# Trace of a batched matrix product: the last batch's twelve rows of A in two loads, and more of the last B on TensorE

## The chip, the core and the metric

The kernel runs on one core of a Trainium2 chip. The metric is the device time in microseconds, the median over several executions. TensorE is called PE here, VectorE DVE, ScalarE ACT, GpSimd POOL and SyncE SP, as the profile calls them.

## The reference

```python
B, N = 8, 2176
a, b: (B, N, N) float32, standard normal

prod = np.matmul(a, b)
traces = np.diagonal(prod, axis1=1, axis2=2).sum(axis=-1)     # (8,) float32
```

The trace of a product is the sum over i and j of a[i, j] * b[j, i]. So no product of matrices has to be made: A is transposed and multiplied element by element with B, and everything is summed. Both inputs must be read whole, 303 MB.

## The kernel before

**Tiles.** N = 2176 is 17 times 128. A "row" below is one of 17 blocks of 128 rows of a matrix. In SBUF a matrix lies as 128 partitions by 17 rows by 2176 columns in bf16; the loads cast from float32. The rows come in three groups: two of six (`SIX`) and one of five (`FIVE`). The tile `five` holds the five rows 12 to 16, first of A and then of B; `a_six` and `b_six` hold the twelve rows 0 to 11 of A and of B; `at` holds A transposed. Within a group of m rows, partition p holds m successive rows of the matrix, so that a load reads one long stretch of memory for each partition and group.

**Loads.** POOL issues nearly all of them, in this order for each batch: A's five rows (`d_a5`), A's twelve (`d_a6`, both groups of six in one DMA), B's five (`d_b5`) and B's twelve (`d_b6`). It waits before each for its buffer to be free: `product` counts DVE's multiplications, `made` counts the tiles that PE has transposed. The last batch's B comes in nine pieces instead (`pieces`), so that the work on it can follow the loads closely: piece 0 is the five rows 12 to 16, piece 1 the rows 0 to 5, piece 2 the rows 6 and 7, pieces 3 to 5 the rows 8, 9 and 10, and pieces 6 to 8 parts of row 11. Each has a semaphore of its own (`d_late`).

**Transposing A.** `tiles` lists the steps: eight for the five rows (`HEAD` is 8), nine for each group of six. A step is up to 16 transposes on PE into one of three slots of PSUM, which ACT (three steps of four) or DVE (each fourth) then copies into `at`. PE runs the steps of all batches in one hardware loop (L217). It waits on the semaphore `moved` ahead of the five rows' first step and ahead of the twelve rows' first. SP posts to `moved`: it waits for the loads `d_a5` and `d_a6` of each batch in turn and adds one for each. So PE's loop needs no waits on counts that change from batch to batch.

**Multiplying.** In batches 0 to 6 DVE multiplies `at` with B and sums, in one instruction for the five rows and one for the twelve (L285, `multiply_reduce`). In the last batch the work is divided between DVE and PE by the list `shares`, with one entry (lo, hi, more) for each piece: DVE multiplies the elements lo to hi, PE takes the rest in steps of 128 columns, as matmuls that add up in `trace_ps` (L254) and whose diagonal is wanted. `more` is a number of extra matmuls of 128x512 into a PSUM slot whose results are not used (L256). PE goes through the pieces in order and waits for each piece's load; it begins once all of A is evacuated. DVE does its parts in order (from L318), each into a column of `late`, then waits for PE's last matmul (`added`), reduces the diagonal of `trace_ps` into a further column (the instruction that writes `diagonal`), PE adds the columns (L334), DVE copies the result (L339) and SP stores it.

Of the kernel before, what the change touches and what calls it, by code (L numbers as in the profile page):

```python
# [21 lines left out]
def kernel(  # L22
# [7 lines left out]
    P = 128  # L30
    BATCH, N, N2 = a.shape
    assert N == N2 and N % P == 0
    NT = N // P
    SIX, FIVE = 6, 5
    TWICE = 2 * SIX
    assert TWICE + FIVE == NT
    LAST = BATCH - 1
# [5 lines left out]
    HALF = 8 * P  # L43
# [5 lines left out]
    at = big.tile([P, NT, N], bf16, tag="at")  # L49
    a_six = big.tile([P, TWICE, N], bf16, tag="a_six")  # L50
# [16 lines left out]
    def tiles_of(rows, start, m):  # L67

        words = rows.bitcast(f32)
        dst = at[:, :, start:start + P * m].rearrange("q v (p r) -> q v p r", r=m)  # L70
        pairs, singles = [], []
        for first, bm in groups:
            v = first // P
            if bm % 2 == 0:
                for t in range(bm // 2):
                    pairs.append((v + 2 * t, first // 2 + t, bm // 2))
            else:
                singles += [(v + r, first + r, bm) for r in range(bm)]
        for v, c0, step in pairs:
            yield (  # L80
                [(f32, r, words[:, r, c0:c0 + step * (P - 1) + 1:step]) for r in range(m)],
                dst[:, v:v + 2, :, :],
                lambda ps: ps[:, 0:m, :].bitcast(bf16).rearrange("q r (p s) -> q s p r", s=2),
            )
        each = 16 // m
        for at0 in range(0, len(singles), each):
            some = singles[at0:at0 + each]
            yield (
                [
                    (bf16, n * m + r, rows[:, r, c0:c0 + step * (P - 1) + 1:step])  # L90
                    for n, (_, c0, step) in enumerate(some) for r in range(m)
                ],
                dst[:, some[0][0]:some[0][0] + len(some), :, :],
                lambda ps, k=len(some): ps.bitcast(bf16).rearrange("q a b -> q (a b)")[
                    :, 0:k * m * P
                ].rearrange("q (n r p) -> q n p r", r=m, p=P),
            )

    six_tiles = [
        t for g in range(2)  # L100
        for t in tiles_of(a_six[:, g * SIX:(g + 1) * SIX, :], g * SIX * P, SIX)
    ]
    five_tiles = list(tiles_of(five, TWICE * P, FIVE))
    tiles = five_tiles + six_tiles
    EACH, HEAD = len(tiles), len(five_tiles)
    on_vector = [n for n in range(EACH) if n % 4 == 3]
    on_scalar = [n for n in range(EACH) if n % 4 != 3]

    def flat(t):
        return t.rearrange("p r k -> p (r k)")  # L110

    def six(src):
        return src[0:TWICE * P, :].rearrange("(g p r) k -> p g (r k)", g=2, r=SIX)

    def rows_of(src, start, m, r0, r1):
        return src[start:start + P * m, :].rearrange("(p r) k -> p (r k)", r=m)[:, r0 * N:r1 * N]

    by_twos = "p (g r) k -> p g (r k)"


    def last_b(v):
        if v < TWICE:
            return b_six[:, v, :]
        return five[:, v - TWICE, :]

    class Piece:
# [14 lines left out]


    shares = [
        (0, N, 0), (0, N, 0), (0, 0, 7), (0, 0, 6), (0, 0, 6), (HALF, N, 2),
        (6 * P, 11 * P, 0), (0, 0, 0), (0, 0, 0),
    ]

    with tc.tile_critical(no_gpsimd_drain=True):
        def counted(name):
            return Counted(nc, name)  # L150

        first_row, unread = counted("first_row"), nc.alloc_semaphore("unread")
        d_a6, d_a5, d_b6, d_b5 = (counted(f"load_{x}") for x in ("a6", "a5", "b6", "b5"))
        d_late = [counted(f"late{n}") for n in range(len(pieces))]
        zeros, ready, cast = counted("zeros"), counted("ready"), counted("cast")
        moved, made = nc.alloc_semaphore("moved"), nc.alloc_semaphore("made")
# [7 lines left out]
        sp = nc.sync  # L164
        words = flat(b_six[:, 0:2, :].bitcast(f32))
        first_row.by(sp.dma_start(out=words, in_=rows_of(a[0], TWICE * P, FIVE, 0, 1)), 16)
        for n in range(BATCH):
            if n == 0:
                sp.wait_ge(cast.sem, 2)
            for load in (d_a5, d_a6):  # L170
                sp.wait_ge(load.sem, 16 * (n + 1))
                sp.sem_inc(moved)


        gp = nc.gpsimd
# [1 line left out]
        def fetch(count, dst, src):  # L177
            count.by(gp.dma_start(out=dst, in_=src), 16)  # L178

        for n in range(BATCH):  # L180
            if n == 0:
                fetch(d_a5, flat(five[:, 1:, :]), rows_of(a[0], TWICE * P, FIVE, 1, FIVE))
                fetch(d_a6, a_six.rearrange(by_twos, g=2), six(a[0]))
                gp.wait_ge(zeros.sem, 2)
                for t in (identity32, identity16):
                    ready.by(gp.affine_select(
                        out=t, in_=t, compare_op=mybir.AluOpType.not_equal, fill=1.0, base=0,
                        pattern=[[-1, P]], channel_multiplier=1,
                    ))
            else:  # L190
                gp.wait_ge(product.sem, 2 * n - 1)
                fetch(d_a5, flat(five), rows_of(a[n], TWICE * P, FIVE, 0, FIVE))
                gp.wait_ge(made, EACH * n)
                fetch(d_a6, a_six.rearrange(by_twos, g=2), six(a[n]))
            gp.wait_ge(made, EACH * n + HEAD)
            if n < LAST:
                fetch(d_b5, flat(five), rows_of(b[n], TWICE * P, FIVE, 0, FIVE))
                if n == 0:
                    gp.wait_ge(cast.sem, 2)
                else:  # L200
                    gp.wait_ge(product.sem, 2 * n)
                fetch(d_b6, b_six.rearrange(by_twos, g=2), six(b[n]))
                continue
            for k, piece in enumerate(pieces):
                if k == 1:
                    gp.wait_ge(product.sem, 2 * n)
                fetch(d_late[k], piece.dst, piece.src)
# [8 lines left out]
            pe.sem_inc(free[k])  # L216
        with pe.Fori(0, BATCH):  # L217
            for n, (moves, _, _) in enumerate(tiles):
                if n in (0, HEAD):
                    pe.wait_ge(moved, 1).then_inc(moved, -1)  # L220
                ps = slots[n % SLOTS]
                pe.wait_ge(free[n % SLOTS], 1).then_inc(free[n % SLOTS], -1)  # L222
                for dtype, place, src in moves:
                    if dtype == f32:
                        last = pe.transpose(ps[:, place, :], src, identity32)  # L225
                    else:
                        ps16 = ps.bitcast(bf16).rearrange("q a b -> q (a b)")
                        last = pe.transpose(ps16[:, place * P:(place + 1) * P], src, identity16)  # L228
                last.then_inc(made, 1)
# [6 lines left out]
        for k, (piece, (lo, hi, more)) in enumerate(zip(pieces, shares)):  # L236
            mine = []
            for v in range(piece.v0, piece.v1):
                row = last_b(v)
                for c in range(piece.lo, piece.hi, P):  # L240
                    if not lo <= c < hi:
                        mine.append((k, at[:, v, c:c + P], row[:, c:c + P]))
            work += mine
            if more:
                x = at[:, piece.v1 - 1, :]
                work += [(k, x[:, 0:P], x[:, 0:4 * P])] * more
        waited, real = -1, [w for w in work if w[2].shape[-1] == P]
        for w in work:
            k, x, y = w
# [34 lines left out]
        def multiply_reduce(x, y, acc, out=None):  # L284
            return dve.tensor_tensor_reduce(  # L285
                out=x if out is None else out, in0=x, in1=y, scale=1.0, scalar=0.0,
                op0=MUL, op1=ADD, accum_out=acc,
            )
# [28 lines left out]
        for k, (piece, (lo, hi, _)) in enumerate(zip(pieces, shares)):  # L317
            if hi > lo:  # L318
                dve.wait_ge(d_late[k].sem, 16)
                t, base = (b_six, 0) if piece.v0 < TWICE else (five, TWICE)  # L320
                if piece.v1 - piece.v0 > 1:
                    x = flat(at[:, piece.v0:piece.v1, :])
                    y = flat(t[:, piece.v0 - base:piece.v1 - base, :])
                else:
                    x, y = at[:, piece.v0, lo:hi], last_b(piece.v0)[:, lo:hi]
                parts.by(multiply_reduce(x, y, late[:, cols:cols + 1]))
                cols += 1
        dve.wait_ge(added.sem, 1)
# [48 lines left out]
```

## Time and profile before

| | |
|---|---|
| median of 3 runs | 711.36 us (711.30 to 711.43) |
| profiled execution | 711.61 us |
| its span, first to last instruction | 709.8 us |
| mean granted clock of PE | 0.653 |
| busy: PE, DVE, ACT, POOL | 207.4, 380.9, 205.1, 24.8 us |
| read from HBM | 303.04 MB, 427 GB/s over the span |
| moved by the core's DMA engines | 152.14 MB, mean 214 GB/s |

The DMA engines' bytes are those written, in bf16; HBM's are those read, in float32. All times in the trace count from the start of the span. The page shows the span in 40 equal slices: on a row of digits each is a busy share in tenths. In the timeline a row gives start and length, engine, line, operation, the tiles written and read, the number of instructions, and in brackets how long the engine had been idle and what ended that. The chain of waits is followed back from the last instruction: start, length, what ran. A DMA row gives the tiles, the queue, the number of issues, their size and the time from issue to landing.

### The profile page before, as it was taken

Reading aid. Unit: us, or ns where it says so; the run is one execution under the profiler, and the core shown is the slowest. Engines: PE = TensorE matmul, PEld = TensorE weight load, DVE = VectorE, ACT = ScalarE, POOL = GpSimd, SP = SyncE. Lnnn points to the kernel's source line nnn. Section 1 sums busy time; section 2 is a strip of 40 time slices with the busy share of each in tenths; the row PEclk is TensorE's granted clock in tenths of the full one; section 3 lists DMA queues with packets and bytes.
Section 4 is the critical chain, followed back from the end, with each engine's and each line's share of the span. In section 5 each row is a group of like instructions: output and inputs, shape, how many; then the busy total and the mean of one; then the engine's idle time right before and its main releaser. Section 6 shows DMA issues by size and latency. Waiting matters only on the chain. (4 is left out here: it accounts for less than half of the span.)

```text
span 709.8 us, 3904 instructions
## 1 busy us (share of the span) xinstructions
PE 207.4 (29%) x1617; PEld 187.4 (26%) x1617; DVE 380.9 (54%) x92; ACT 205.1 (29%) x162; POOL 24.8 (3%) x45
## 2 busy tenths in 40 slices
PE   0335003450134401244013530125201362012717
PEld 0335002340124301243013420125201251012615
DVE  0105487154971639716396163951739427393288
ACT  1427002470034600436004440045400463004720
POOL 1000000000000000000000000000000000002000
PEclk9859555685556855668556775556755576556767
DMA  9999999999999999999999999999999999999995
GB/s 233 215 216 219 216 206 222 221 208 219 219 214 217 221 211 229 212 209 230 206 225 221 206 219 215 217 218 220 213 219 220 213 226 212 216 223 212 218 206 113
DMA packets 7688, 152.14 MB, mean 214 GB/s; under 512 B 643, under 2 KB 899, under 8 KB 1411
## 3 DMA queue, kind: packets, MB, share of 16 engines
q0 software_dynamic: 7536, 150.96, 99.2%
q1 hardware_dynamic: 146, 1.11, 0.4%
q8 instruction: 2, 0.03, 0.0%
q14 instruction: 4, 0.02, 0.0%
HBM read 303.04 MB, written 0.00 MB: 427 GB/s over the span
## 5 line engine op out<-in xcount | busy, mean ns | idle before, releaser
L270 ACT COPY at<-aT 128x1536 bf16<-128x1536 bf16 (+3 forms) x160 | 202.7, 1358 | 469.6 <-DVE sums L285 355.7
L285 DVE CUSTOM_DVE_ANT_0 at<-at,b_six 128x26112 bf16<-128x26112 bf16 (+3 forms) x10 | 207.3, 20743 | 82.1 <-DMA b_six<-in_b_dram 82.1
L296 DVE COPY at<-aT 128x1536 bf16<-128x1536 bf16 (+1 forms) x48 | 80.1, 1669 | 222.2 <-PE aT L225 170.8
L225 PE MATMUL aT<-identity,five 128*128 128x128 f32 x240 | 55.0, 419 | 367.9 <-PEq L222 367.9
L225 PEld LDWEIGHTS aT<-identity,five 128*128 128x128 f32 x240 | 47.3, 221 | 373.8 <-issue 373.8
L225 PE MATMUL aT<-identity,a_six 128*128 128x128 f32 x576 | 91.8, 325 | 104.3 <-PEq L222 104.1
L225 PEld LDWEIGHTS aT<-identity,a_six 128*128 128x128 f32 x576 | 85.7, 206 | 110.0 <-issue 109.8
L285 DVE CUSTOM_DVE_ANT_0 at<-at,five 128x10880 bf16<-128x10880 bf16 x8 | 91.9, 11491 | 14.3 <-ACT at L270 14.3
L228 PE MATMUL aT<-identity,a_six 128*128 128x128 bf16 x480 | 33.6, 219 | 11.7 <-PEq L222 11.7
L228 PEld LDWEIGHTS aT<-identity,a_six 128*128 128x128 bf16 x480 | 29.4, 118 | 15.7 <-issue 15.7
L228 PE MATMUL aT<-identity,five 128*128 128x128 bf16 x200 | 16.9, 258 | 0.0
L228 PEld LDWEIGHTS aT<-identity,five 128*128 128x128 bf16 x200 | 16.6, 132 | 0.4
L178 POOL DMA_DIRECT2D five<-in_b_dram x8 | 4.5, 563 | 334.5 <-PE aT L228 334.5
L178 POOL DMA_DIRECT2D five<-in_a_dram x8 | 4.6, 577 | 294.4 <-DVE sums L285 293.4
L254 PE MATMUL trace_ps<-b_six,at 128*128 128x128 bf16 x88 | 7.5, 254 | 14.4 <-DMA b_six<-in_b_dram 14.4
L254 PEld LDWEIGHTS trace_ps<-b_six,at 128*128 128x128 bf16 x88 | 6.9, 116 | 15.5 <-issue 14.7
L178 POOL DMA_DIRECT2D b_six<-in_b_dram x15 | 9.2, 636 | 0.0
L256 PE MATMUL aT<-at 128*128 128x512 bf16 x21 | 6.4, 445 | 0.0
L178 POOL DMA_DIRECT2D a_six<-in_a_dram x8 | 5.7, 711 | 0.0
L282 DVE CAST five<-b_six 128x1088 bf16<-128x1088 f32 x1 | 0.7, 727 | 4.6 <-DMA b_six<-in_a_dram 4.6
L256 PEld LDWEIGHTS aT<-at 128*128 128x128 bf16 x21 | 2.2, 114 | 2.3 <-issue 1.4
L263 ACT CAST five<-b_six 128x1088 bf16<-128x1088 f32 x1 | 1.1, 1100 | 3.8 <-DMA b_six<-in_a_dram 3.8
(17 smaller groups left out, 6.2 us busy)
## 6 DMA issues: line engine op xcount, KB each, us to landing
a_six<-in_a_dram POOLq DMA_DIRECT2D x8, 6528.0 KB, 54.7
b_six<-in_b_dram POOLq DMA_DIRECT2D x7, 6528.0 KB, 52.1
five<-in_b_dram POOLq DMA_DIRECT2D x8, 2720.0 KB, 22.0
five<-in_a_dram POOLq DMA_DIRECT2D x7, 2720.0 KB, 24.5
b_six<-in_b_dram POOLq DMA_DIRECT2D x1, 3264.0 KB, 37.4
five<-in_a_dram POOLq DMA_DIRECT2D x1, 2176.0 KB, 14.7
b_six<-in_b_dram POOLq DMA_DIRECT2D x3, 544.0 KB, 46.9
b_six<-in_a_dram SPq DMA_DIRECT2D x1, 1088.0 KB, 5.0
```

The lines of the kernel that those rows point to most:

```text
L178: count.by(gp.dma_start(out=dst, in_=src), 16)
L225: last = pe.transpose(ps[:, place, :], src, identity32)
L228: last = pe.transpose(ps16[:, place * P:(place + 1) * P], src, identity16)
L254: ins = pe.matmul(trace_ps, x, y, start=w is real[0], stop=w is real[-1])
L256: pe.matmul(slots[0][:, 0:4, :], x, y, start=True, stop=True)
L263: cast.by(act.copy(out=five[:, 0, :middle], in_=words[:, :middle]))
L270: ins = act.copy(out=dst, in_=view(slots[t % SLOTS]))
L282: cast.by(dve.tensor_copy(out=five[:, 0, middle:], in_=words[:, middle:]))
L285: return dve.tensor_tensor_reduce(out=x if out is None else out, in0=x, in1=y, scale=1.0, scalar=0.0, op0=MUL, op1=ADD, accum_out=acc,)
L296: ins = dve.tensor_copy(out=dst, in_=view(slots[t % SLOTS]))
```

## The change

For the last batch, A's twelve rows come by two loads, one for each group of six, the second with a semaphore of its own (`d_a12`). PE waits on `moved` a third time in each batch, ahead of the second group's first step (`NECK`); SP posts that third one right after the second in batches 0 to 6, and after the second load in the last.

The list `shares` is new for pieces 0, 1, 4 and 5. DVE's part of a piece of several rows can now end within the piece, and PE's steps are compared with it accordingly. Piece 0 stays whole on DVE. Of piece 1 DVE keeps the rows 0 to 2, and PE takes the rows 3 to 5 and 7 extra matmuls. Row 9, which PE did, becomes DVE's; its 6 extra matmuls stay. Of rows 10 and 11 DVE keeps what it had. The extra matmuls read row 11 of `at` in all pieces.

```diff
     EACH, HEAD = len(tiles), len(five_tiles)
+    NECK = HEAD + len(six_tiles) // 2
...
     shares = [
-        (0, N, 0), (0, N, 0), (0, 0, 7), (0, 0, 6), (0, 0, 6), (HALF, N, 2),
+        (0, FIVE * N, 0), (0, 3 * N, 7), (0, 0, 7), (0, 0, 6), (0, N, 6), (HALF, N, 2),
         (6 * P, 11 * P, 0), (0, 0, 0), (0, 0, 0),
     ]
...
+        d_a12 = counted("load_a12")
...
-            for load in (d_a5, d_a6):
-                sp.wait_ge(load.sem, 16 * (n + 1))
-                sp.sem_inc(moved)
+            sp.wait_ge(d_a5.sem, 16 * (n + 1))
+            sp.sem_inc(moved)
+            sp.wait_ge(d_a6.sem, 16 * (n + 1))
+            sp.sem_inc(moved)
+            if n == LAST:
+                sp.wait_ge(d_a12.sem, 16)
+            sp.sem_inc(moved)
...
                 gp.wait_ge(made, EACH * n)
-                fetch(d_a6, a_six.rearrange(by_twos, g=2), six(a[n]))
+                if n < LAST:
+                    fetch(d_a6, a_six.rearrange(by_twos, g=2), six(a[n]))
+                else:
+                    for g, load in enumerate((d_a6, d_a12)):
+                        fetch(
+                            load, flat(a_six[:, g * SIX:(g + 1) * SIX, :]),
+                            rows_of(a[n], g * SIX * P, SIX, 0, SIX),
+                        )
...
-                if n in (0, HEAD):
+                if n in (0, HEAD, NECK):
                     pe.wait_ge(moved, 1).then_inc(moved, -1)
...
-                    if not lo <= c < hi:
+                    if not lo <= (v - piece.v0) * N + c < hi:
                         mine.append((k, at[:, v, c:c + P], row[:, c:c + P]))
...
-                x = at[:, piece.v1 - 1, :]
+                x = at[:, TWICE - 1, :]
...
-                if piece.v1 - piece.v0 > 1:
-                    x = flat(at[:, piece.v0:piece.v1, :])
-                    y = flat(t[:, piece.v0 - base:piece.v1 - base, :])
-                else:
-                    x, y = at[:, piece.v0, lo:hi], last_b(piece.v0)[:, lo:hi]
+                x = flat(at[:, piece.v0:piece.v1, :])[:, lo:hi]
+                y = flat(t[:, piece.v0 - base:piece.v1 - base, :])[:, lo:hi]
```

## The prediction

> **What bounds the kernel now.** I read the page first: where the DMA engines stop, and who ends last.
>
> ```profile
> span 709.8 us, 3904 instructions
> DMA  9999999999999999999999999999999999999995
> GB/s 233 215 216 219 216 206 222 221 208 219 219 214 217 221 211 229 212 209 230 206 225 221 206 219 215 217 218 220 213 219 220 213 226 212 216 223 212 218 206 113
> ```
>
> The DMA engines are full in 39 of 40 slices of 17.7 us and half full in the last, so everything up to the last loads is a matter of bytes, and the change moves no byte. What can be won lies between the last landing and the end. The DMA issues, asked in narrow windows, give the time from issue to landing of each load; the timeline gives the issues.
>
> ```profile
> 649.22 0.56 POOL L178 DMA_DIRECT2D five<-in_b_dram  x1 [44.26 <-PE aT L228]
> five<-in_b_dram POOLq DMA_DIRECT2D x1, 2720.0 KB, 22.6
> 649.78 4.25 POOL L178 DMA_DIRECT2D b_six<-in_b_dram  x8
> b_six<-in_b_dram POOLq DMA_DIRECT2D x1, 3264.0 KB, 37.4
> b_six<-in_b_dram POOLq DMA_DIRECT2D x1, 1088.0 KB, 42.1
> b_six<-in_b_dram POOLq DMA_DIRECT2D x1, 544.0 KB, 44.2
> b_six<-in_b_dram POOLq DMA_DIRECT2D x3, 544.0 KB, 46.9
> b_six<-in_b_dram POOLq DMA_DIRECT2D x1, 544.0 KB, 48.4
> b_six<-in_b_dram POOLq DMA_DIRECT2D x1, 352.0 KB, 49.6
> b_six<-in_b_dram POOLq DMA_DIRECT2D x1, 128.0 KB, 49.7
> b_six<-in_b_dram POOLq DMA_DIRECT2D x1, 64.0 KB, 49.6
> ```
>
> Eight issues in 4.25 us start about 0.52 apart (649.78, 650.30, 650.83, 651.35, 651.87, 652.39, 652.91, 653.43). With their times the pieces of the last B land: piece 0 (rows 12 to 16) 671.8, piece 1 (rows 0 to 5) 687.2, piece 2 (6, 7) 692.4, row 8 at 695.0, row 9 at 698.25 (46.9 is the median of the three, its own), row 10 at 700.3, the three parts of row 11 at 702.0, 702.6 and 703.0. So the last byte is there at 703.0. Then the chain of waits, in order of time, and the timeline of DVE and PE:
>
> ```profile
> 669.53 0.94 PE aT L225 x6
> 670.50 8.87 ACT at L270 x7
> 679.66 11.41 DVE at L285
> 691.08 13.67 DVE at L285
> 704.76 1.27 DVE at L285
> 706.03 0.74 DVE at L285
> 692.50 3.78 PE L254 MATMUL trace_ps<-b_six,at 128*128 128x128 bf16 x34 [14.42 <-DMA b_six<-in_b_dram]
> 696.08 2.85 PE L256 MATMUL aT<-at 128*128 128x512 bf16 x7
> 698.77 1.11 PE L254 MATMUL trace_ps<-b_six,at 128*128 128x128 bf16 x17
> 699.72 1.46 PE L256 MATMUL aT<-at 128*128 128x512 bf16 x6
> 701.01 1.11 PE L254 MATMUL trace_ps<-b_six,at 128*128 128x128 bf16 x17
> 704.13 0.83 PE L254 MATMUL trace_ps<-b_six,at 128*128 128x128 bf16 x12
> 706.70 0.28 DVE L285 CUSTOM_DVE_ANT_0 diagonal<-identity,trace_ps 128x128 bf16<-128x128 f32 x1
> ```
>
> The end hangs on DVE: it waits for A's last transposes and ACT's evacuations, starts piece 0 at 679.66 though that landed at 671.8, and then runs without a gap. The reduction of PE's sum (`diagonal`) starts at 706.70, 3.7 us after the last landing. From there to the end of the span are 3.1 us that the change leaves alone (its sixth column adds one tiny matmul, issued before the last wait).
>
> PE isn't far behind. It runs without a gap from 692.50 to 704.13 + 0.83 = 704.96: the last twelve matmuls, whose data was complete at 703.0, start at 704.13. DVE cut alone would bring the reduction to 705.0 and no earlier.
>
> **The change, part by part.** *DVE's share.* Piece 0 stays whole (11.41). Of piece 1 DVE keeps three of six rows, 6528 of 13056 elements. The chain gives 1.27 us for 1152 elements, 0.74 for 640 and 13.67 for 13056, so (13.67 - 1.27)/(13056 - 1152) = 1.042 ns for each further element: 6528 take 6.87, and row 9, now DVE's whole (2176), takes 2.34. Rows 10 (1.27) and 11 (0.74) keep their parts. In all 11.41 + 6.87 + 2.34 + 1.27 + 0.74 = 22.6 against 27.1.
>
> *PE's share.* It gains 51 matmuls of rows 3 to 5 and loses row 9's 17; the filler matmuls of 128x512 go from 21 to 28. So 122 matmuls and 28 fillers, in the order 51, 7, 34, 7, 17, 6, 6, 8, 2, 12, the first waiting for piece 1 (687.2), where before the first waited for piece 2 (692.4). Their price depends on the clock:
>
> ```profile
> 684.00:687.20 3.20, 0.00 (x0) 0.00 (x0) 3.20 (x1) 0.00 (x0) 0.00 (x0) 0.50 0.73 152
> 692.50:698.40 5.90, 5.90 (x40) 4.47 (x41) 5.90 (x1) 0.00 (x0) 0.00 (x0) 0.50 1.05 213
> 698.50:704.90 6.40, 6.40 (x71) 4.47 (x70) 6.40 (x3) 0.00 (x0) 0.00 (x0) 1.00 0.56 100
> ```
>
> Of the last columns of these windows the first is the granted clock: 0.50 while PE idled before piece 1's landing, still 0.50 for the first 5.9 us of matmuls, 1.00 after. At 0.50 34 matmuls took 696.08 - 692.50, or 0.105 each; at 1.00 17 took 699.72 - 698.77, or 0.056 each, and a filler (701.01 - 699.72)/6 = 0.215; twice that, 0.43, at half clock. I take the same 5.9 us of half clock from 687.3, that is to 693.2. The 51 end at 687.3 + 5.4 = 692.7, one filler is slow, six take 1.3: 694.4. The 34 (landed) end at 696.3, seven fillers 697.8, row 8's 17 (landed) 698.8, 12 fillers 701.4 (the second six wait for row 9, 698.25, long past), row 10's eight 701.8, two fillers 702.3. Row 11's twelve would end at about 703.2 if their data were there, and the last two must wait for 703.0. PE then ends with the last landing: 0.1 from landing to matmul (692.4 to 692.50), two starts at 0.056, and the last one's duration (0.83 - 11 x 0.056 = 0.21): 703.4.
>
> The Trainium skill, TensorE: Matmul & The Clock Gate (Why this matters for your kernels), says that a pause of over 3 us drops the array to half rate and that about 4 us of steady work restores it, which speaks against handing rows to a PE that has just rested. The trace agrees on the drop, but 5.9 us went by here; with 4 us the stream would still end with the last landing.
>
> *DVE's line.* Piece 0 at 671.9 to 683.3; piece 1's half 687.3 to 694.2; row 9 from 698.35 to 700.7; row 10 to 702.0; row 11's part 702.1 to 702.8. So DVE waits 0.6 us for PE, and the reduction starts at about 703.45.
>
> *A's twelve rows by two loads.* That line needs piece 0 started early. Before:
>
> ```profile
> 603.68 0.56 POOL L178 DMA_DIRECT2D five<-in_a_dram  x1 [39.54 <-DVE sums L285]
> 604.24 0.71 POOL L178 DMA_DIRECT2D a_six<-in_a_dram  x1
> a_six<-in_a_dram POOLq DMA_DIRECT2D x1, 6528.0 KB, 54.7
> five<-in_a_dram POOLq DMA_DIRECT2D x1, 2720.0 KB, 24.5
> 659.30 6.74 PE L225 MATMUL aT<-identity,a_six 128*128 128x128 f32 x36 [10.38 <-PEq L222]
> 646.57 4.02 ACT L270 COPY at<-aT 128x1280 bf16<-128x1280 bf16 x3 [0.36 <-PE aT L225]
> 615.32 27.36 DVE L285 CUSTOM_DVE_ANT_0 at<-at,b_six 128x26112 bf16<-128x26112 bf16 x1 [11.94 <-DMA b_six<-in_b_dram]
> ```
>
> The load landed at 604.24 + 54.7 = 658.9, behind A's five rows (603.68 + 24.5 = 628.2), so its first half should be there at 643.6. Transposes and evacuations of both halves took 659.3 to 679.4, the first nine tiles 10.2 us (to the 669.53 of the chain). Now the first nine can follow the five rows' evacuation (646.57 + 4.02 = 650.6) and end at 660.8; the second half, there at 658.9, ends at 670.7, before piece 0 lands. Should they run 2 or 3 us longer on a slower clock, piece 0 still ends before 687.2: 3.9 us of cover. Without the split at all, piece 0 ends at 691.1, DVE's half of piece 1 at 698.0, and row 9 isn't there until 698.25. So with the new shares the split buys only margin; I put it at 0. With the old shares it would buy 1.7 (the reduction at PE's 705.0).
>
> The split adds one issue on POOL, 0.71 us at most, ahead of the five rows of B; POOL then idles 44.26 us before issuing those, which hides it. If that cover went, it would cost the 0.71. SP waits for one load more before its output DMA, some 45 us ahead of that. PE's third wait per batch (at NECK) is met at once in batches 0 to 6; bounds 0 and 0.1 us, hidden because DVE waits 11.94 us for B's load anyway; I take 0.
>
> As to the loads themselves, 1088 KB took 692.4 - 687.2 = 5.2 and the 544 KB behind it 2.6: half the bytes, half the time, so a queued load costs nothing of its own, with at most 0.1 for rounding.
>
> The Trainium skill, DMA: Bandwidth & Descriptors (Anatomy of one DMA), gives each DMA a fixed 2.0 us, mostly the receipt after the last byte, which is against splitting a load. If that held the engines up here, the gain would be 1.2 us; by the rows above, loads in a queue overlap it.
>
> **The sum.** Reduction at 703.45 for 706.70: -3.25. I take 3.2, span 706.6. The profiled execution took 711.61, 1.81 beyond its span, and the median of the runs is 711.36; so 708.4 for such a profile and 711.36 - 3.2 = 708.2 for the median, 0.45% less.
>
> **Rivals.** *PE's clock stays down, slower* (chance 0.05). All 122 x 0.105 + 28 x 0.43 = 24.9 us at half clock from 687.3 end at 712.2, the reduction 5.5 later than before: 716.9. It decides from the point where PE ends at 706.7, 19.4 us after the start; all at full clock is 12.9, so that needs 13 us of half clock. For it: the change gives the bounding end to an engine at 0.50. Against: 5.9 us was enough before, and the fillers keep PE busy.
>
> *The clock comes late* (0.07): with 9.4 us at half clock for 5.9, the 3.5 us more cost PE 1.75 behind its 703.4: 709.9.
>
> *DVE becomes the bound* (0.10): it has 0.6 us in hand behind row 9, whose landing (3.2 after row 8, beside 2.6 for the same bytes) already wobbles. A landing 2 us later puts its parts of rows 9, 10 and 11 at 700.35 to 704.7, and the time at 709.4.
>
> *The split costs DMA time* (0.05): the engines stand still between A's two loads until the first one's completion is in, and everything behind lands later. The price of a DMA with nothing in it is in SP's waits, in all, times, longest:
>
> ```profile
> SPq L148 <- DMA out_dram<-result: 0.7, 1, 0.7
> ```
>
> The output's 32 bytes are waited for 0.7 us. All landings 0.7 later give 708.9; there is no gain left once the last landing slips 3.2. For it: two completions where there was one. Against: the 5.2 and 2.6 above. (By the fixed time of the Trainium skill, DMA: Bandwidth & Descriptors, Anatomy of one DMA, it would be 710.2.)
>
> *The change does not do what it says* (0.03): the two halves of A share the engines and land together at 658.9. Then DVE starts piece 0 at 679.66 as before, and by the sum above the time is still 708.2.
>
> **How the numbers follow.** The forecast itself has 0.70: 708.2, its own range 707.6 to 708.8 (landings 0.4 either way; PE's half clock shorter than 5.9 us or up to 1 us longer, which moves its end by 0.4). The range goes from 707.5 over the DVE and DMA cases and the earlier part of the late clock to 709.6. About 0.2%, 1.4 us, is what a measurement of this kernel can tell from no change: faster by that means below 709.94. Forecast, DVE, DMA and unsplit cases and a little under half of the late clock, which lies on that border: 0.91 faster; the rest of the late clock 0.04 same; 0.05 slower.
>
> **What would show it.** Right: a first-half transpose near 649 to 651, DVE's piece 0 at 671.9, PE's 51 matmuls from 687.3, PE and DVE both waiting for row 11's load, `diagonal` at 703.3 to 703.8 with the last landing at 703. Wrong: a last landing later than 703.5, a granted clock of 0.50 beyond 695, or a DVE that reaches `diagonal` after PE.

## The result, and the profile after

The median goes from 711.43 us (5 runs, 711.30 to 712.0) to 708.23 (5 runs, 708.10 to 708.64), 3.2 us less; the ratio is 0.9953, 95% interval 0.9939 to 0.9968. The prediction was 708.2, between 707.5 and 709.6. The profiled execution took 708.64, the longest of its five, with a span of 706.9, 2.9 less than before.

The page of the changed kernel, the rows that answer to those of before:

```profile
span 706.9 us, 4009 instructions
DMA  9999999999999999999999999999999999999997
GB/s 222 228 207 212 229 212 213 217 223 214 220 221 213 206 229 213 213 215 226 209 228 216 210 221 215 214 213 226 215 220 220 214 206 229 207 217 222 220 207 150
```

The DMA engines are as full as they were; of the row of digits the last slice alone changes, from 5 tenths to 7, with 150 GB/s for 113. The same bytes, and less time without any at the end. POOL's timeline at the issues, the DMA issues in windows as narrow (size, time from issue to landing), and a row of SP's waits (in all, times, longest):

```profile
649.81 0.53 POOL L184 DMA_DIRECT2D five<-in_b_dram  x1 [44.23 <-PE aT L241]
...
650.33 0.55 POOL L184 DMA_DIRECT2D b_six<-in_b_dram  x1
...
653.97 0.61 POOL L184 DMA_DIRECT2D b_six<-in_b_dram  x1
```

```profile
five<-in_b_dram POOLq DMA_DIRECT2D x1, 2720.0 KB, 21.9
...
b_six<-in_b_dram POOLq DMA_DIRECT2D x1, 3264.0 KB, 36.8
...
b_six<-in_b_dram POOLq DMA_DIRECT2D x1, 64.0 KB, 49.4
```

```profile
SPq L178 <- DMA a_six<-in_a_dram: 15.4, 1, 15.4
```

Piece 0 lands at 649.81 + 21.9 = 671.7, piece 1 at 650.33 + 36.8 = 687.1 and the last part of row 11 at 653.97 + 49.4 = 703.4. Before these were 671.8, 687.2 and 703.0. SP's new wait (L178) shows that A's second half really comes 15.4 us after its first. Then the end of the chain of waits, and the timeline of the tail:

```profile
653.45 49.63 DMA b_six<-in_b_dram
703.08 0.05 issue
703.13 0.61 PE trace_ps L267 x6
703.74 0.02 issue
703.76 0.29 DVE diagonal L298
```

```profile
649.35 0.89 PE L238 MATMUL aT<-identity,a_six 128*128 128x128 f32 x6
660.17 8.86 ACT L283 COPY at<-aT 128x1536 bf16<-128x1536 bf16 x7 [0.66 <-PE aT L238]
671.72 11.49 DVE L298 CUSTOM_DVE_ANT_0 at<-at,five 128x10880 bf16<-128x10880 bf16 x1 [2.39 <-DMA five<-in_b_dram]
687.13 6.96 DVE L298 CUSTOM_DVE_ANT_0 at<-at,b_six 128x6528 bf16<-128x6528 bf16 x1 [3.91 <-DMA b_six<-in_b_dram]
687.24 5.60 PE L267 MATMUL trace_ps<-b_six,at 128*128 128x128 bf16 x51 [19.48 <-DMA b_six<-in_b_dram]
698.10 2.43 DVE L298 CUSTOM_DVE_ANT_0 at<-at,b_six 128x2176 bf16<-128x2176 bf16 x1 [4.00 <-DMA b_six<-in_b_dram]
702.48 0.83 DVE L298 CUSTOM_DVE_ANT_0 at<-at,b_six 128x640 bf16<-128x640 bf16 x1 [0.40 <-DMA b_six<-in_b_dram]
702.50 1.22 PE L267 MATMUL trace_ps<-b_six,at 128*128 128x128 bf16 x12 [0.18 <-DMA b_six<-in_b_dram]
703.76 0.29 DVE L298 CUSTOM_DVE_ANT_0 diagonal<-identity,trace_ps 128x128 bf16<-128x128 f32 x1 [0.45 <-PE trace_ps L267]
```

Before, the chain ended in 27 us of DVE without a gap. Now its last long link is a load, and the brackets show waits for loads behind piece 0: DVE waits 3.91 us for piece 1, 4.00 for row 9 and 0.40 for row 11, PE 0.18 for row 11. At the end DVE waits 0.45 us for PE. The reduction starts 0.4 us after the last landing, where it was 3.7.

### The profile page after: what moved, and what is told of

The parts are those of the page before. It is cut to its first block, busy times and chain, and to the rows that moved or that the text cites. A ratio compares the mean times of both kernels' runs of the same rounds, so it can differ in the third digit from the quotient of the medians.

```text
span 706.9 us, 4009 instructions
## 1 busy us (share of the span) xinstructions
PE 208.3 (29%) x1660; PEld 187.5 (27%) x1660; DVE 376.9 (53%) x94; ACT 204.8 (29%) x162; POOL 25.1 (4%) x46
## 5 line engine op out<-in xcount | busy, mean ns | idle before, releaser
L298 DVE CUSTOM_DVE_ANT_0 at<-at,b_six 128x26112 bf16<-128x26112 bf16 (+4 forms) x11 | 203.1, 18461 | 90.8 <-DMA b_six<-in_b_dram 90.8
L238 PE MATMUL aT<-identity,a_six 128*128 128x128 f32 x576 | 90.0, 319 | 96.4 <-PEq L235 96.3
L238 PEld LDWEIGHTS aT<-identity,a_six 128*128 128x128 f32 x576 | 83.7, 205 | 102.2 <-issue 102.1
L267 PE MATMUL trace_ps<-b_six,at 128*128 128x128 bf16 x122 | 10.5, 259 | 19.8 <-DMA b_six<-in_b_dram 19.7
L267 PEld LDWEIGHTS trace_ps<-b_six,at 128*128 128x128 bf16 x122 | 9.6, 120 | 21.3 <-issue 19.6
## 6 DMA issues: line engine op xcount, KB each, us to landing
b_six<-in_b_dram POOLq DMA_DIRECT2D x1, 3264.0 KB, 36.8
```

What stands on the lines that cost most here:

```text
L267: ins = pe.matmul(trace_ps, x, y, start=w is real[0], stop=w is real[-1])
L298: return dve.tensor_tensor_reduce(out=x if out is None else out, in0=x, in1=y, scale=1.0, scalar=0.0, op0=MUL, op1=ADD, accum_out=acc,)
```

## The experiments

The runs were made in three groups, each on a chip of its own with the kernel before beside it; a ratio is always to those. Its medians there were 711.31 us (beside the shares alone, the split alone, the change without unused matmuls and the split in all batches), 711.53 (beside the split alone and the kernel before, each without its unused matmuls, row 9 back on PE and seven more unused matmuls) and 711.66 (beside the changed kernel run again, the shares alone without unused matmuls and the sixteen for 28). So a few tenths between runs of different groups say little. The "unused matmuls" are the prediction's fillers.

**The shares alone.** The new `shares`, A's twelve rows in one load.

```diff
-            if n == LAST:
-                sp.wait_ge(d_a12.sem, 16)
...
-                if n < LAST:
-                    fetch(d_a6, a_six.rearrange(by_twos, g=2), six(a[n]))
-                else:
...
+                fetch(d_a6, a_six.rearrange(by_twos, g=2), six(a[n]))
```

> The change with A's twelve rows in one load, as before; the new shares stay. My theory (shares bring the whole gain, the split only margin): DVE starts piece 0 at about 679.7 and ends it at 691.1, ends its half of piece 1 at 698.0, before row 9 lands at 698.1 to 698.3; the reduction still starts with PE's last matmul after the last landing. Median 708.2, within 0.3 of the changed kernel. Rival (the split is needed, DVE late otherwise): DVE reaches row 9 late and the reduction waits for DVE, 708.8 or more.

Measured: 708.31 (708.19 to 708.52), ratio 0.9956, interval 0.9943 to 0.997. The whole gain. DVE's timeline:

```profile
679.24 11.48 DVE L288 CUSTOM_DVE_ANT_0 at<-at,five 128x10880 bf16<-128x10880 bf16 x1
690.65 6.95 DVE L288 CUSTOM_DVE_ANT_0 at<-at,b_six 128x6528 bf16<-128x6528 bf16 x1
697.66 2.42 DVE L288 CUSTOM_DVE_ANT_0 at<-at,b_six 128x2176 bf16<-128x2176 bf16 x1
703.31 0.29 DVE L288 CUSTOM_DVE_ANT_0 diagonal<-identity,trace_ps 128x128 bf16<-128x128 f32 x1 [0.55 <-PE trace_ps L257]
```

Piece 0 starts at 679.24, 7.5 us later than in the changed kernel, and DVE still waits 0.55 us for PE at the end: the time that the split won was time in which DVE would wait. Its only waits behind piece 0 are 0.34 us for row 11 and this one.

**The split alone.** A's load in two, the shares of before.

```diff
-        (0, FIVE * N, 0), (0, 3 * N, 7), (0, 0, 7), (0, 0, 6), (0, N, 6), (HALF, N, 2),
+        (0, FIVE * N, 0), (0, 6 * N, 0), (0, 0, 7), (0, 0, 6), (0, 0, 6), (HALF, N, 2),
```

> The change with the shares of before; A's twelve rows still by two loads. My theory: DVE starts piece 0 at 671.7 and has everything done by about 703.2, but PE starts only with piece 2 at 692.4 to 693.0 and ends at 705.0 as before; the reduction then starts at 705.0, 1.7 earlier than before: 709.7. Rival A (the start of DVE was all that mattered): 708.2 as the whole change. Rival B (the split brings nothing at all): 711.4.

Measured: 708.85, ratio 0.9965 (0.9953 to 0.9978), and six executions far apart: 708.45, 708.58, 708.62, 709.09, 710.14, 710.21. The profiled one is that of 710.14; its timeline and its windows (the granted clock is the third number from the end):

```profile
692.69 3.79 PE L267 MATMUL trace_ps<-b_six,at 128*128 128x128 bf16 x34 [24.69 <-DMA b_six<-in_b_dram]
702.34 0.82 DVE L298 CUSTOM_DVE_ANT_0 at<-at,b_six 128x640 bf16<-128x640 bf16 x1
704.36 0.83 PE L267 MATMUL trace_ps<-b_six,at 128*128 128x128 bf16 x12
705.23 0.29 DVE L298 CUSTOM_DVE_ANT_0 diagonal<-identity,trace_ps 128x128 bf16<-128x128 f32 x1 [2.06 <-PE trace_ps L267]
```

```profile
692.70:698.60 5.90, 5.90 (x40) 4.49 (x41) 5.90 (x1) 0.00 (x0) 0.00 (x0) 0.50 1.06 214
698.80:705.10 6.30, 6.30 (x70) 4.45 (x68) 4.37 (x6) 0.00 (x0) 0.00 (x0) 1.00 0.52 93
```

This execution does what was expected: DVE is done by 703.2 and waits 2.06 us for PE, whose clock rose after 5.9 us, as before. But four of six ended 1 to 1.7 us earlier. A clock that rose 2 to 3.4 us sooner would save PE half of that, which is the distance; there is no profile of these four, so for them that is argued. The next run takes away the work on which such a clock would act.

**The split alone, without the unused matmuls.** As the last, with other numbers of unused matmuls:

```diff
-        (0, FIVE * N, 0), (0, 6 * N, 0), (0, 0, 7), (0, 0, 6), (0, 0, 6), (HALF, N, 2),
+        (0, FIVE * N, 0), (0, 6 * N, 0), (0, 0, 0), (0, 0, 0), (0, 0, 0), (HALF, N, 0),
```

> The split of A's load with the shares of before and none of the 21 unused matmuls. My theory (with the shares of before, the unused matmuls at a clock that rises at a moment of its own are what made PE late): 88 matmuls take 9.2 us at half clock and wait for row 11's landing: 708.6, and executions that agree within 0.2. Rival (PE is late for its rows): 708.9 or more, and executions as far apart as with the unused matmuls (708.5 to 710.2).

Measured: 708.41 (708.12 to 708.54), ratio 0.9954 (0.9941 to 0.9968). PE's rows in its timeline:

```profile
692.71 4.30 PE L267 MATMUL trace_ps<-b_six,at 128*128 128x128 bf16 x51 [24.71 <-DMA b_six<-in_b_dram]
698.34 1.12 PE L267 MATMUL trace_ps<-b_six,at 128*128 128x128 bf16 x17 [1.33 <-DMA b_six<-in_b_dram]
700.40 0.62 PE L267 MATMUL trace_ps<-b_six,at 128*128 128x128 bf16 x8 [0.94 <-DMA b_six<-in_b_dram]
702.15 1.45 PE L267 MATMUL trace_ps<-b_six,at 128*128 128x128 bf16 x12 [1.13 <-DMA b_six<-in_b_dram]
```

The same rows on the same engines, and PE waits about a microsecond for row 9, for row 10 and for row 11. The executions agree within 0.4 us, where 0.2 was expected and the split alone had 1.8. So it was the 21 unused matmuls that made PE late with the shares of before, not its rows of B. It also means that the old division of rows, with the split and without unused matmuls, comes as far as the new one.

**The kernel before, without its unused matmuls.** Nothing else is changed:

```diff
-        (0, N, 0), (0, N, 0), (0, 0, 7), (0, 0, 6), (0, 0, 6), (HALF, N, 2),
+        (0, N, 0), (0, N, 0), (0, 0, 0), (0, 0, 0), (0, 0, 0), (HALF, N, 0),
```

> The kernel before without its 21 unused matmuls. My theory (DVE bounds it, its last product ends 1.7 us behind PE): 711.3 as before. Rival (PE holds up the end there too): 710 or less.

Measured: 711.26, ratio 0.9997 (0.9988 to 1.0006): no difference. The timeline:

```profile
702.76 0.64 PE L254 MATMUL trace_ps<-b_six,at 128*128 128x128 bf16 x6 [0.17 <-DMA b_six<-in_b_dram]
705.70 0.82 DVE L285 CUSTOM_DVE_ANT_0 at<-at,b_six 128x640 bf16<-128x640 bf16 x1
706.44 0.28 DVE L285 CUSTOM_DVE_ANT_0 diagonal<-identity,trace_ps 128x128 bf16<-128x128 f32 x1
```

PE is done at 703.4, and the reduction comes at 706.44 behind DVE's last product. Before, DVE held up the end. Beside this run, on the same chip, the split took the same shares without unused matmuls from 711.26 to 708.41.

**The change without unused matmuls.**
```diff
-        (0, FIVE * N, 0), (0, 3 * N, 7), (0, 0, 7), (0, 0, 6), (0, N, 6), (HALF, N, 2),
+        (0, FIVE * N, 0), (0, 3 * N, 0), (0, 0, 0), (0, 0, 0), (0, N, 0), (HALF, N, 0),
```

> The change without any of the 28 matmuls of 128x512 whose results are not used. My theory (the end is the last landing): 122 matmuls fit even at half clock, 122 x 0.105 = 12.8 us from 687.2, and PE waits at every piece. If the clock falls back to 0.50 the last matmuls cost 0.1 to 0.2 us more: 708.2 to 708.5. Rival (the fillers are needed, as the clock would otherwise make PE late): over 709.

Measured: 708.56 (708.49 to 708.60), ratio 0.9959 (0.9945 to 0.9972), 0.3 above the changed kernel, which ran in another group. Its windows, and a row of its chain:

```profile
687.60:691.30 3.70, 3.70 (x36) 3.70 (x37) 3.70 (x1) 0.00 (x0) 0.00 (x0) 0.50 0.99 207
691.40:698.10 6.70, 4.14 (x68) 3.63 (x65) 3.28 (x3) 0.00 (x0) 0.00 (x0) 1.00 1.04 210
698.20:703.60 5.40, 2.41 (x20) 1.89 (x20) 4.27 (x6) 0.00 (x0) 0.00 (x0) 0.50 0.72 131
```

```profile
702.22 1.48 PE trace_ps L267 x12
```

The clock does fall to 0.50 at 698.2, and row 11's twelve matmuls take 1.48 us for 1.22. Here a half clock at the end costs 0.2 to 0.3 us. That is an estimate from these two durations and the medians: the changed kernel's profiled execution, the longest of its five, took as long (708.64) as this one (708.60). The rival's 5.5 us supposed a half clock throughout and had the fillers in it, 12 of 24.9 us; the clock rose after 3.7 us here.

**The shares alone, without unused matmuls.** The edits of the shares alone and of the last run together.

> The new shares alone: A's twelve rows in one load, no unused matmuls. My theory (the shares carry the gain, the rest is margin): within 0.3 of the changed kernel beside it, and 0.2 of that for matmuls of row 11 at half clock. Rival (the three parts of the change need each other): 709 or more.

Measured: 708.46 (708.45 to 708.57), ratio 0.9956 (0.9943 to 0.997), beside 708.21 for the changed kernel run again on the same chip (708.14 to 708.40, ratio 0.9953, 0.9939 to 0.9967). Of that last it was expected:

> The changed kernel once more, beside the next two on the same chip: 708.2 to 708.6 (708.23 when it was first measured).

So a new division of rows, without the split and without unused matmuls, has all but 0.25 us of the gain.

**Row 9 back on PE.**

```diff
-        (0, FIVE * N, 0), (0, 3 * N, 7), (0, 0, 7), (0, 0, 6), (0, N, 6), (HALF, N, 2),
+        (0, FIVE * N, 0), (0, 3 * N, 7), (0, 0, 7), (0, 0, 6), (0, 0, 6), (HALF, N, 2),
```

> The change, with row 9 back on PE (17 matmuls more for PE, 2.4 us less for DVE). My theory (PE has a few tenths in hand, DVE is not the bound): 17 x 0.056 = 0.95 us more in a stream that waited 0.2 to 0.7 us in all for row 11: 708.4 to 709.0. Rival (DVE is the bound): 708.1 or less.

Measured: 708.71 (708.37 to 709.0), ratio 0.996 (0.9947 to 0.9974). PE's 17 matmuls come out of its margin and, by the median, a little more; DVE, 2.4 us lighter, gives nothing back. DVE isn't the bound. The profile is that of a 708.37, in which PE's clock rose after 3.7 us and the reduction started at 703.50.

**Seven more unused matmuls.**

```diff
-        (0, FIVE * N, 0), (0, 3 * N, 7), (0, 0, 7), (0, 0, 6), (0, N, 6), (HALF, N, 2),
+        (0, FIVE * N, 0), (0, 3 * N, 14), (0, 0, 7), (0, 0, 6), (0, N, 6), (HALF, N, 2),
```

> The change with 14 matmuls of 128x512 behind piece 1's rows in place of 7. My theory (past the few tenths in hand, PE's work goes to the end one for one): 7 x 0.215 = 1.5 us at full clock, up to 3.0 at half, less 0.2 to 0.7: 709.0 to 710.7, by where in the stream the clock rises. Rival (the last landing alone decides): 708.3.

Measured: 708.66 (708.39 to 709.38), ratio 0.9958 (0.9944 to 0.9971): less than expected. The profile is that of the 709.38:

```profile
687.30:692.60 5.30, 5.30 (x51) 5.30 (x52) 5.30 (x1) 0.00 (x0) 0.00 (x0) 0.50 0.99 206
692.70:704.30 11.60, 11.60 (x108) 7.37 (x106) 6.09 (x8) 0.00 (x0) 0.00 (x0) 1.00 0.84 164
```

Here the clock rose after 5.3 us and PE ran without a gap to the end; this one is as expected. The rest ended earlier: by the sum of 1.5 us, PE had over a microsecond in hand in the 708.39, more than the 0.2 to 0.7 us that profiles show. A clock that rose earlier would give it. In the split in all batches, where PE has the changed kernel's work behind A, the clock rose after 4.2 us and PE waited 0.48 and 0.20 us for row 11's loads, where the changed kernel's profile has 5.6 and 0.18. For the 708.39 itself there is no profile.

**Sixteen unused matmuls for 28.**

```diff
-        (0, FIVE * N, 0), (0, 3 * N, 7), (0, 0, 7), (0, 0, 6), (0, N, 6), (HALF, N, 2),
+        (0, FIVE * N, 0), (0, 3 * N, 0), (0, 0, 4), (0, 0, 5), (0, N, 5), (HALF, N, 2),
```

> The change with 16 unused matmuls in place of 28: none behind piece 1, then 4, 5, 5 and 2. My theory (the end is the last landing, PE needs only to be in time and at full clock then): PE comes to row 11 early whatever the phase of the clock, 0.0 to 0.2 less than the changed kernel beside it, and executions no further apart. If the clock falls before 703: 0.2 more.

Measured: 708.59 (708.11 to 709.43), ratio 0.9957 (0.9944 to 0.9971): no better, against what was expected. The 709.43 was no longer on the core: its span is 706.5 us, and 2.9 us lie outside the span, where the changed kernel's executions have 1.7 to 1.8. The spans, 706.3 to 706.8, are no further apart than the changed kernel's, 706.3 to 706.9. In its profile (an execution of 708.78) the twelve last matmuls take 1.48 us, as without any. No version run here beats the changed kernel by more than the executions differ.

**The split in all batches.** A's twelve rows by two loads in each of the eight batches.

```diff
-            if n == LAST:
-                sp.wait_ge(d_a12.sem, 16)
+            sp.wait_ge(d_a12.sem, 16 * (n + 1))
...
-                fetch(d_a6, a_six.rearrange(by_twos, g=2), six(a[0]))
+                for g, load in enumerate((d_a6, d_a12)):
...
-                if n < LAST:
-                    fetch(d_a6, a_six.rearrange(by_twos, g=2), six(a[n]))
-                else:
-                    for g, load in enumerate((d_a6, d_a12)):
...
+                for g, load in enumerate((d_a6, d_a12)):
...
```

> The change with A's twelve rows by two loads in all eight batches, seven splits more. My theory (a load queued behind others costs nothing of its own, at most 0.1 each): 708.2, at most 708.9. Rival (a load's completion is exposed between the two, 0.7 each by the output's landing): 713.1. By the 2.0 us of the Trainium skill, DMA: Bandwidth & Descriptors, Anatomy of one DMA, if it were not overlapped: 722.

Measured: 708.49 (708.30 to 708.54), ratio 0.9958 (0.9944 to 0.9971): 0.3 above the changed kernel's two medians for seven splits more, about 0.04 each; as those ran in other groups, even that may be chance. The 713.1 of the rival is ruled out. The fixed 2.0 us of the Trainium skill, DMA: Bandwidth & Descriptors (Anatomy of one DMA), doesn't show for a load that has another queued behind it.

## Why the prediction was right

**The bound.** "The end hangs on DVE" held: without its unused matmuls PE ended 1.6 us earlier and the kernel before took 711.26 all the same. After the change the last landing decides, as forecast: DVE and PE both wait for row 11. That "DVE cut alone" would stop at PE's 705.0 wasn't run as such; in the split alone it is what the profiled execution did, while four others ended earlier.

**DVE's durations and line.** 6.87 and 2.34 us were worked out for 6528 and 2176 elements; 6.96 and 2.43 stand in the timeline, which has the read of the sum within it (13.75 there for the 13.67 of the chain). Piece 0 started at 671.72 for 671.9, row 9's part at 698.10 for 698.35.

**PE's line.** Started at 687.24 for 687.3. Half clock was taken over from the profile of before at 5.9 us; it was 5.6:

```profile
687.30:692.90 5.60, 5.60 (x52) 5.49 (x53) 5.60 (x1) 0.00 (x0) 0.00 (x0) 0.50 1.00 208
693.00:703.10 10.10, 9.82 (x93) 6.17 (x91) 5.52 (x7) 0.00 (x0) 0.00 (x0) 1.00 0.95 184
```

PE waited for row 11's landing, as forecast, with 0.2 us in hand ahead of row 11's twelve matmuls. The last landing was 703.4 for 703.0 in this execution, and the reduction at 703.76 for 703.45; the span 706.9 for 706.6 differs by the same 0.3. This profile was the longest of five executions; in the one of the second measurement, 708.14, the reduction started at 703.26. So the working is right to some 0.3 us, and that the median agrees to 0.03 us is luck: the executions lie 0.5 us apart.

**The split.** "with the new shares the split buys only margin; I put it at 0": 708.31 against 708.23. A's last transposes were evacuated at 660.17 + 8.86 = 669.0 for 670.7.

**What was mis-sized.** "With the old shares it would buy 1.7": it bought 2.5 in the median and 1.1 in the slowest execution. The step took PE's end of 705.0 for a fixed time. But PE's stretch held the 21 unused matmuls, and without them PE waited for each load and the split bought 2.85. Why the split alone ended early in four of six executions and late in two stays open. A clock that rises at another moment in each execution would do it, but no kernel here was profiled with two such moments. Before, none of this mattered, because DVE ended later still.

**The rivals.** The clock didn't stay down and didn't come late: it rose 2.7 to 6.0 us after PE's first matmul in all profiles, where the late case had 9.4. DVE didn't become the bound: with 2.4 us less on DVE the time was no shorter. The split's price of 0.7 came out at about 0.04. The two halves of A didn't land together: SP waited 15.4 us between them.

## What to carry to other kernels

When loads run without a gap to the end, look at what starts after the last landing, engine by engine: here DVE was 3.7 us behind it and PE 2.0, and giving PE three rows of an earlier piece for one of a later, so that it started 5.3 us sooner, took nearly all of it. Where the trace shows an engine waiting for data after a step, making that step start earlier buys nothing; with the new shares the split of A's load was such a step. With the old ones, where DVE ran without a gap to the end, the same split bought 2.85 us (711.26 to 708.41, both without unused matmuls). What a part of a change is worth depends on the rest: the new shares alone, or the split with the unused matmuls left out, each brought nearly the whole gain. A filler that keeps a clock up is itself work: with the shares of before the 21 fillers made PE later and the executions uneven, with the new ones the 28 are worth about 0.3 us by the medians.

## What the runs showed of the hardware

The time from PE's first matmul of the tail to the rise of its clock doesn't follow from PE's work in the tail. It was 5.9 us in the kernel before, 5.6 in the changed one, 5.9 in the split alone and 3.7 in the change without fillers; in the split alone without fillers it was 2.7:

```profile
692.70:695.40 2.70, 2.69 (x26) 2.70 (x27) 2.70 (x1) 0.00 (x0) 0.00 (x0) 0.50 1.05 213
695.50:702.20 6.70, 3.29 (x53) 2.78 (x51) 6.70 (x3) 0.00 (x0) 0.00 (x0) 1.00 1.00 190
```

In all of these PE had no pause in that stretch. Runs with the same work on PE behind A differ: 2.7 us here and 3.8 in the kernel before without its unused matmuls (a granted clock of 0.50 to 696.3, 1.00 from 696.5), on the same chip; on another, 6.0 in the shares alone (0.50 to 693.3, 1.00 from 693.5) and 4.2 in the split in all batches, whose windows are

```profile
687.40:691.40 4.00, 4.00 (x39) 4.00 (x40) 4.00 (x1) 0.00 (x0) 0.00 (x0) 0.50 0.95 199
691.60:701.60 10.00, 10.00 (x100) 6.53 (x98) 6.22 (x5) 0.00 (x0) 0.00 (x0) 1.00 1.06 207
```

The changed kernel, the only one profiled twice, had 5.6 both times, so that the moment differs between executions of one kernel is not shown. The Trainium skill, TensorE: Matmul & The Clock Gate (Why this matters for your kernels), has at least 4 us of steady work; these runs lie on both sides of that. A time from one profile is not one to build a sum on.

Seven more splits of a queued load of 6.5 MB cost 0.3 us in all, by medians of different groups.
